# A decoder layer with sparse and dilated attention: six edits to what TensorE reads, and when

## The chip, the cores and the metric

One core of a Trainium2 chip runs the whole layer as one program. Its engines are TensorE (PE in the profile: matrix products, with its weight loads shown as PEld), VectorE (DVE), ScalarE (ACT), GpSimd (POOL) and SyncE (SP), which starts most DMA transfers. The metric is the device time of one execution in microseconds (us), the median of several runs.

## The reference, cut to what matters

The layer works on 512 tokens of 1024 channels, in float32: a half-step feed-forward block, a token mixer, and a second half-step feed-forward block, each between RMS norms.

```python
def token_mixer(h, ...):
    proj = h @ w_in                         # queries, keys, values, gates of all branches
    o_nsa = nsa_attention(...)              # compressed + selected + window branch, 8 heads
    o_dil = dilated_attention(...)          # 3 groups of 4 heads, dilation 1, 4, 16
    y_nsa = o_nsa.reshape(B, S, Q_NSA) @ w_nsa_o
    y_dil = o_dil.reshape(B, S, DIL_OUT) @ w_dil_o
    y = jax.nn.sigmoid(g_a) * y_nsa + jax.nn.sigmoid(g_b) * y_dil
    return y @ w_mix_out

def nsa_attention(...):
    ...
    p_cmp, _ = masked_softmax(s_c, dist_c >= 0)     # 31 compressed blocks
    o_cmp = jnp.einsum('bgrsc,bcgd->bsgrd', p_cmp, vc)
    ...
    return g[..., 0:1] * o_cmp + g[..., 1:2] * o_slc + g[..., 2:3] * o_win

def reference(x, ...):
    h = rms_norm(x, ffn1_pre)
    x = x + 0.5 * rms_norm(swiglu(h, ffn1...), ffn1_post)
    h = rms_norm(x, mix_pre)
    x = x + rms_norm(token_mixer(h, ...), mix_post)
    h = rms_norm(x, ffn2_pre)
    return x + 0.5 * rms_norm(swiglu(h, ffn2...), ffn2_post)
```

With 512 tokens all eight selected blocks are chosen, so the selected branch is plain causal attention, as the window branch is: the kernel runs two causal heads ("branches", br = 0 and 1) for each of 8 query heads, and a small compressed head beside them.

## The kernel before, in words

**Products.** Each float32 product is made of three matmuls in the 4-byte format fp32r: both operands are split into a high part (a cast on ScalarE, line 163) and the rest (a subtraction on VectorE, line 164), and `mm3` (lines 208 to 210) adds high times high, high times rest and rest times high. In the profile a matmul is written out<-moving,stationary. The stationary operand is loaded into the array ahead of its matmul (PEld); the moving operand streams through it, up to 512 columns. With `turn=True` the moving operand's two halves are read in turn, column 0 of the first half, column 0 of the second, and so on; the result then stands in that order in PSUM and is put right by the strided read of whoever takes it out (`from_turn`).

**Order of the work.** The program is traced in Python order; a scheduler then orders each engine's instructions by their place in the trace and by what its own model of time finds ready. `issue_after(i)` keeps what is traced in its block behind instruction i on i's engine; it is an order, not a wait. Tiles of one tag share a fixed number of buffers ("slots"); a new tile waits until an older one is read for the last time. The tag SP has 11 slots, raw (weights as they come from memory) 3, and PSUM's eight banks are shared as S 3, T 2, V 1, F 2.

**Sparse branch** (`nsa`, about 365 to 510 us). Sixteen turns n take one pair of head and branch each; the work of a turn is drawn out over three turns (LAG = 2). At every fourth turn two heads' queries are projected and split (`q_parts`). `cmp_pair` makes the compressed branch of two heads: 8 small score matmuls (line 1211), a softmax on VectorE and ScalarE, 4 transposes (line 1232), a split. `hb_probs` scales and transposes the probabilities of turn n - 2 (line 1275) into bank T and splits them into PT slots, in three portions: key tile 0, then key tiles 1 and 3 together, then key tile 2. `hb_scores` makes the scores of turn n into bank S (lines 1013 and 1014) and their softmax rows. `hb_values` (line 1290) multiplies values and probabilities of turn n - 2 for the key tiles 0, 1, 2, 3, of 512, 384, 256 and 128 query columns, once for the high part and once for the rest. At the second branch one more matmul (line 1364) adds the compressed branch, and `fold` (lines 1298 and 1299) adds the two 64-row halves of the bank. Units of the merge gates' projection are put between as filler.

**Dilated branch** (`dil`, about 510 to 698 us). Group 0 has dilation 1; groups 1 and 2 run on tokens in residue order, token 4n + r at place r, n. Queries and keys come from "lots" of block products (`lot_blocks`), whose summed operands (`mix_token_sums`) are held in the SP slots. The values of group 0 are projected from 620 us; those of groups 1 and 2 follow as one loop over eight k: the stationary operand is a quarter of the tokens, read with a step of four elements straight out of the normed input:

```python
xs = [x[k0 + j].rearrange("p (n r) -> p r n", r=4) for x in (self.xh, self.xl)]
for t in range(NT):
    self.mm3(banks[t], xs[0][:, t], xs[1][:, t], w[0][:, j], w[1][:, j], ...)
```

Meanwhile `factors` makes each group's share from the softmax sums (lines 1719 to 1734), and GpSimd scales all probabilities by it (line 1747). Then twelve items, four heads by three groups, are transposed (`transposed`, lines 1799 and 1812), split into SP slots, multiplied by the values (`values`, lines 1826 and 1827 for group 0, 1834 for the others) and added up (line 1839); the sparse branch's output products are filler between them. `dil_weights(0)`, the split of the first half of w_dil_o, is traced behind all items.

**End.** `ffn_down` ends with the rows of token tile 3: a square on ScalarE (line 216), the factor on VectorE and GpSimd (lines 225 and 229), the gain (line 955), two updates of 512 columns (line 927), and two stores of 256 KB on SP's queue (line 2139).

Of the kernel before, what the change touches and what calls it, by code (L numbers as in the profile page):

```python
# [17 lines left out]
OP = mybir.AluOpType  # L18
# [66 lines left out]
class Layer:  # L85
# [110 lines left out]
    def halves(self, v):  # L196

        return v.rearrange("p (h a c) -> p h a c", h=2, a=2)

    def rows_of(self, v):  # L200
# [553 lines left out]
    def ffn_down(self, first, E, later, kept, wd, td, post, finish, xsrc, aside, opened):  # L754
# [200 lines left out]
        nc.vector.tensor_mul(c[1], c[1], gain[0][0])  # L955
        update(3, (c[1], c22[1]), r)
        finish(3, gain[1])

# [327 lines left out]
    def hb_values(self, probs, br, half, out, first):  # L1286
        for kk in range(NT):
            v = self.vn[kk][:, 2 * br + half].rearrange("p h d -> p (h d)")
            for pi, pp in enumerate(probs[kk]):
                self.nc.tensor.matmul(out[:, kk * P:S], v, pp, start=first and kk == 0 and pi == 0, stop=False,  # L1290
                                      skip_group_check=True)

# [8 lines left out]
    def nsa(self, fillers, sums):  # L1301
# [32 lines left out]
        for n in range(len(heads) + LAG):  # L1334
            if n < len(heads) and n % 4 == 0:
                i = n // 4
                b, _ = self.proj_T(None, None, None, wq) if i == 0 else self.proj_T(self.wcols([(i * 64, 64), (256 + i * 64, 64)]))
                qs[i] = self.q_parts(b)
                if i:
                    cmps[i] = self.cmp_pair(i, qs[i])  # L1340
            m = n - LAG
# [4 lines left out]
            if n < len(heads):  # L1346
                i, half, br = heads[n]
                h = i + 4 * half
                if br == 0:
                    ws[h] = self.slot("W")  # L1350
                    nc.vector.tensor_scalar(ws[h], self.dm, -(2.0 ** -(h + 1)), None, op0=OP.mult)
                kb, ka = kparts[br]
                live[n] = self.hb_scores(qs[i][half], ka[half], kb, half, ws[h])
            if m >= 0:
                i, half, br = heads[m]
                with self.tc.issue_after(self.last_pool):
                    sums(m)
                if br == 0:
                    out = self.bank("V")
                    if half == 0:  # L1360
                        of = self.slot("x")
                self.hb_values(probs.pop(m), br, half, out, br == 0)
                if br == 1:
                    nc.tensor.matmul(out, self.vcs[half], cmps[i], start=False, stop=True, skip_group_check=True)
                    self.fold(of, half, out[0:64], out[64:128])
                    if half == 1:
                        self.oh.append(of)
# [190 lines left out]
    def dil(self, fillers, early_gates):  # L1558
# [216 lines left out]
        for k0 in range(0, KT, 2):  # L1775
            if k0 % 4 == 0:
                r = self.raw(wv[:, k0:k0 + 4], [4, S])
            w = self.wsplit(r[:, k0 % 4:k0 % 4 + 2], [2, S])
            if k0 == 2:
                factors()  # L1780
            for j in range(2):
                xs = [x[k0 + j].rearrange("p (n r) -> p r n", r=4) for x in (self.xh, self.xl)]
                for t in range(NT):
                    self.mm3(banks[t], xs[0][:, t], xs[1][:, t], w[0][:, j], w[1][:, j], k0 + j == 0, k0 + j == KT - 1,
                             turn=True)
# [34 lines left out]
        def values(g, hh, pieces, acc):  # L1820

            mm = nc.tensor.matmul
            if g == 0:
                out = self.bank("V")
                for n, (kk, qc, hi, lo) in enumerate(pieces):
                    mm(out[:, qc], value(g, kk, hh), hi, start=n == 0, stop=False, skip_group_check=True)
                    self.last_value = mm(out[:, qc], value(g, kk, hh), lo, start=False, stop=n == NT - 1, skip_group_check=True).ins
                nc.scalar.copy(acc, out)
                return
            for m, both in enumerate(pieces):  # L1830
                out = self.bank("S")
                for n in range(2):
                    c = slice(n * 256, (n + 1) * 256)
                    self.last_value = mm(out[:, c], value(g, 2 * m + n, hh), both[:, n].rearrange("p x q -> p (x q)"), start=True,
                                         stop=True).ins
                av = acc.rearrange("p (n r) -> p n r", r=4)[:, :, 2 * m:2 * m + 2]
                ov = out.rearrange("p (r x n) -> p x n r", r=2, x=2)
                for x in range(2):
# [11 lines left out]

        self.dh, self.dl = [], []
        items = [(hh, g) for hh in range(4) for g in range(3)]
        pend = {}
        for n in range(len(items) + 1):
            if n < len(items):
                hh, g = items[n]
                pend[n] = transposed(g, hh)
            with self.tc.issue_after(self.last_value if n == len(items) else self.last_trans):
                for _ in range(2 if n == 0 else 1):
# [31 lines left out]
    def mixer(self, post, finish, sums):  # L1891
# [89 lines left out]

        dil_weights(0)
        for d in range(KT):
# [137 lines left out]
    def run(self, out):  # L2121
        nc, a = self.nc, self.a
        self.xdram = self.tc.dram_tile([S, D], F32, name="xdram")
        self.x2dram = self.tc.dram_tile([S, D], F32, name="x2dram")
        NP = NF // 2
# [77 lines left out]
```

## Time and profile before

| | before |
|---|---|
| median of 3 runs | 1083.85 us (1083.21 to 1085.04) |
| the profiled execution | 1083.9 us, span 1081.8 us |
| TensorE busy, weight loads | 1060.2 us (98%), 974.6 us |
| VectorE, ScalarE, GpSimd busy | 915.0, 667.9, 246.4 us |
| mean granted clock of TensorE | 0.999 |
| memory read and written | 214.73 and 74.50 MB |

The span runs from the first to the last instruction of the program; the execution's own time is a little longer. Busy times of TensorE include the time that a matmul needs to run out of the array, which overlaps the next one, so the distance between starts says more than the busy share. In the groups, "x32 | 15.0, 478 | 2.2 <-ACT" is the count, the busy time in us, the mean duration in ns, and the idle time ahead of the group with what ended it. In the timeline each row has its start and its duration in us.

### The profile page before, as it was taken

How to read it: one execution, taken by the hardware profiler on the slowest of the kernel's cores; microseconds unless marked ns; L12 is line 12 of the kernel's file. 1: busy time of each engine (PE TensorE's matmuls, PEld its weight loads, DVE VectorE, ACT ScalarE, POOL GpSimd, SP SyncE). 2: the span in 40 equal slices, each digit the busy share in tenths (PEclk: the TensorE clock that was granted, in tenths of full speed). 3: DMA queues.
4: the chain of work that ended last, by engine and by line, in shares of the span. 5: the costliest groups of instructions: out<-in, count | busy, mean ns of one | idle time of the engine just before them, and what ended most of it. 6: DMA issues, size and time to landing. Idle time of an engine off the chain costs nothing. (4 is left out here: it accounts for less than half of the span.)

```text
span 1081.8 us, 19360 instructions
## 1 busy us (share of the span) xinstructions
PE 1060.2 (98%) x7166; PEld 974.6 (90%) x7166; DVE 915.0 (85%) x1563; ACT 667.9 (62%) x1196; POOL 246.4 (23%) x345
## 2 busy tenths in 40 slices
PE   9999999999999999999999999999999999999997
PEld 7899999988889977777899998888999999998886
DVE  6999999998787988787996746996888999989775
ACT  7465555567675777676797745754445555668462
POOL 0434445410021054454110039001101111000001
PEclk9999999999999999999999999999999999999999
DMA  9899999999962577886766642574387988579862
GB/s 351 259 273 312 284 299 294 303 315 351 355 225 87 195 263 174 263 187 204 166 196 224 206 119 99 180 263 162 131 276 203 261 248 229 152 248 301 301 203 105
DMA packets 87871, 250.65 MB, mean 232 GB/s; under 512 B 11777, under 2 KB 16993, under 8 KB 85089
## 3 DMA queue, kind: packets, MB, share of 16 engines
q1 hardware_dynamic: 67152, 180.40, 48.4%
q0 software_dynamic: 20192, 68.72, 25.5%
q8 instruction: 56, 0.92, 0.3%
q10 hardware_dynamic: 432, 0.30, 0.1%
q14 instruction: 39, 0.31, 0.1%
HBM read 214.73 MB, written 74.50 MB: 267 GB/s over the span
## 5 line engine op out<-in xcount | busy, mean ns | idle before, releaser
L164 DVE TENSOR_TENSOR wlo<-raw,whi 128x1024 fp32r<-128x1024 f32 (+1 forms) x216 | 261.8, 1217 | 79.9 <-ACT whi L163 77.2
L163 ACT CAST whi<-raw 128x1024 fp32r<-128x1024 f32 (+1 forms) x216 | 223.8, 1040 | 95.3 <-PE pb_F L209 17.2
L208 PE MATMUL pb_F<-xhl_t,whi 128*128 128x256 f32 (+1 forms) x320 | 104.7, 327 | 2.0 <-DVE KA_s L996 1.0
L209 PE MATMUL pb_F<-xhl_t,whi 128*128 128x256 f32 (+1 forms) x320 | 103.1, 322 | 0.0
L210 PE MATMUL pb_F<-xhl_t,wlo 128*128 128x256 f32 (+1 forms) x320 | 103.1, 322 | 0.0
L208 PE MATMUL pb_S<-xhl_t,whi 128*128 128x256 f32 (+1 forms) x280 | 82.2, 294 | 0.0
L209 PE MATMUL pb_S<-xhl_t,whi 128*128 128x256 f32 (+1 forms) x280 | 82.1, 293 | 0.0
L210 PE MATMUL pb_S<-xhl_t,wlo 128*128 128x256 f32 (+1 forms) x280 | 82.1, 293 | 0.0
L229 POOL TENSOR_TENSOR rs_t<-rs_t,mhalf_t 128x1 f32<-128x1 f32 x20 | 13.3, 666 | 249.5 <-DVE rs_t L225 249.5
L208 PEld LDWEIGHTS pb_F<-xhl_t,whi 128*128 128x128 f32 x320 | 61.0, 191 | 6.1 <-issue 1.6
L210 PEld LDWEIGHTS pb_F<-xhl_t,wlo 128*128 128x128 f32 x320 | 61.0, 190 | 3.3
L209 PEld LDWEIGHTS pb_F<-xhl_t,whi 128*128 128x128 f32 x320 | 61.0, 191 | 3.0 <-issue 0.2
L1266 POOL TENSOR_SCALAR SP_s<-SP_s,st_t 128x384 f32<-128x384 f32 (+2 forms) x48 | 49.1, 1053 | 55.5 <-PE pb_T L1232 11.6
L209 PE MATMUL pb_T<-xhl_t,whi 128*128 128x256 f32 x216 | 59.4, 275 | 0.0
L210 PE MATMUL pb_T<-xhl_t,wlo 128*128 128x256 f32 x216 | 59.4, 275 | 0.0
L208 PE MATMUL pb_T<-xhl_t,whi 128*128 128x256 f32 x216 | 59.4, 275 | 0.0
L163 ACT CAST whi<-tmp_t 128x1024 fp32r<-128x1024 f32 x36 | 36.5, 1057 | 30.2 <-DVE tmp_t L582 26.6
L210 PEld LDWEIGHTS pb_S<-xhl_t,wlo 128*128 128x128 f32 x280 | 53.6, 191 | 1.3
L208 PEld LDWEIGHTS pb_S<-xhl_t,whi 128*128 128x128 f32 x280 | 53.6, 191 | 1.3
L209 PEld LDWEIGHTS pb_S<-xhl_t,whi 128*128 128x128 f32 x280 | 53.6, 191 | 1.3
L208 PE MATMUL pb_T<-SP_s,whi 128*128 128x256 f32 x176 | 48.8, 277 | 1.5 <-ACT ring_s L1539 1.0
L210 PE MATMUL pb_T<-SP_s,wlo 128*128 128x256 f32 x176 | 48.7, 277 | 0.0
(930 smaller groups left out, 3713.4 us busy)
## 6 DMA issues: line engine op xcount, KB each, us to landing
raw<-in_gu_dram SPq DMA_DIRECT2D x64, 512.0 KB, 5.8
raw<-tdram SPq DMA_DIRECT2D x40, 512.0 KB, 5.0
PT_s<-in_d_dram POOLq DMA_DIRECT2D x66, 256.0 KB, 6.9
raw<-in_d_dram SPq DMA_DIRECT2D x30, 512.0 KB, 5.1
tdram<-in_d_dram POOLq DMA_DIRECT2D x18, 768.0 KB, 10.4
ldram<-in_w_in_dram POOLq DMA_DIRECT2D x12, 1024.0 KB, 10.5
tdram<-PT_s POOLq DMA_DIRECT2D x44, 256.0 KB, 5.9
raw<-in_w_in_dram SPq DMA_DIRECT2D x11, 1024.0 KB, 4.9
```

Of the source, the lines that this page charges most:

```text
L163: self.last_cast = self.nc.scalar.copy(dsthi, src).ins
L164: self.last_sub = self.nc.vector.tensor_sub(dstlo, src, dsthi.bitcast(F32)).ins
L208: mm(out, lhi, rhi, start=start, stop=False, skip_group_check=skip)
L209: mm(out, lhi, rlo, start=False, stop=False, skip_group_check=skip)
L210: self.last_mm = mm(out, llo, rhi, start=False, stop=stop, skip_group_check=skip).ins
L229: nc.gpsimd.tensor_tensor(out=r, in0=v, in1=self.mhalf, op=OP.pow)
L1266: self.last_pool = nc.gpsimd.tensor_scalar(pp, pp, st[:, 1, t:t + 1], None, op0=OP.mult).ins
```

## The change

Six edits, all to order or layout; the values computed are the same.

- **Tokens in residue order.** The two stationary operands of each k of the value projection of groups 1 and 2 are copied by ScalarE into SP slots in residue order, 16 copies of 128 x 512, and the matmuls read the copies.
- **Two rows in turn.** The probabilities of `hb_values`, of the compressed branch and of `values` are read as two rows in turn (in `hb_values` and group 0 the two halves of each tile of 128 columns, 64 elements apart; in groups 1 and 2 the high part and the rest, 128 apart). The outputs are unpicked where PSUM is read.
- **Value tile order.** `hb_values` takes the key tiles in the order 0, 1, 3, 2.
- **Compressed branch.** `cmp_pair` of the later head pairs is traced behind `hb_scores` of its turn instead of ahead of `hb_probs`.
- **Weight split.** The cast and the subtraction of `dil_weights(0)` are put behind those of the third item from the end as traced (`piece[-3]`, the tenth of twelve).
- **Last stores.** In the second feed-forward block the last token tile is updated in four pieces of 256 columns, second half first, each stored at once, on SP's and ScalarE's queues in turn.

```diff
@@ -196,6 +196,22 @@
     def halves(self, v):
 
         return v.rearrange("p (h a c) -> p h a c", h=2, a=2)
+
+    def tiles(self, v):
+
+        return v.rearrange("p (t a c) -> p t a c", a=2, c=64)
+
+    def tiles_in_turn(self, v):
+
+        return v.rearrange("p (t a c) -> p t c a", a=2, c=64)
+
+    def tiles_turned(self, v):
+
+        return v.rearrange("p (t c a) -> p t c a", a=2, c=64)
+
+    def tiles_from_turn(self, v):
+
+        return v.rearrange("p (t c a) -> p t a c", a=2, c=64)
 
     def rows_of(self, v):
 
@@ -953,8 +969,16 @@
         product(half(parts["O"], 256), "T4", None, c, False, True, settle, 6, list(HOLD_TAGS), between)
         r = factor(3, [square(3, c[1]), ms[3, 1]])
         nc.vector.tensor_mul(c[1], c[1], gain[0][0])
-        update(3, (c[1], c22[1]), r)
-        finish(3, gain[1])
+        if opened:
+            update(3, (c[1], c22[1]), r)
+            finish(3, gain[1])
+            return
+        for h, y in ((1, c22[1]), (0, c[1])):
+            x = self.x[6 + h]
+            for i in range(2):
+                o = slice(i * 256, (i + 1) * 256)
+                nc.vector.scalar_tensor_tensor(x[:, o], y[:, o], r, x[:, o], op0=OP.mult, op1=OP.add)
+                (nc.sync, nc.scalar)[i].dma_start(self.last_rows[:, h * S + i * 256:h * S + (i + 1) * 256], x[:, o])
 
 
     def wcols(self, segs):
@@ -1284,11 +1308,11 @@
         return out
 
     def hb_values(self, probs, br, half, out, first):
-        for kk in range(NT):
+        for kk in (0, 1, 3, 2):
             v = self.vn[kk][:, 2 * br + half].rearrange("p h d -> p (h d)")
             for pi, pp in enumerate(probs[kk]):
-                self.nc.tensor.matmul(out[:, kk * P:S], v, pp, start=first and kk == 0 and pi == 0, stop=False,
-                                      skip_group_check=True)
+                self.nc.tensor.matmul(self.tiles_turned(out[:, kk * P:S]), v, self.tiles_in_turn(pp),
+                                      start=first and kk == 0 and pi == 0, stop=False, skip_group_check=True)
 
     def fold(self, dst, half, top, bot):
 
@@ -1336,8 +1360,6 @@
                 i = n // 4
                 b, _ = self.proj_T(None, None, None, wq) if i == 0 else self.proj_T(self.wcols([(i * 64, 64), (256 + i * 64, 64)]))
                 qs[i] = self.q_parts(b)
-                if i:
-                    cmps[i] = self.cmp_pair(i, qs[i])
             m = n - LAG
             if m >= 0:
                 i, half, br = heads[m]
@@ -1351,6 +1373,8 @@
                     nc.vector.tensor_scalar(ws[h], self.dm, -(2.0 ** -(h + 1)), None, op0=OP.mult)
                 kb, ka = kparts[br]
                 live[n] = self.hb_scores(qs[i][half], ka[half], kb, half, ws[h])
+            if n < len(heads) and n % 4 == 0 and n:
+                cmps[n // 4] = self.cmp_pair(n // 4, qs[n // 4])
             if m >= 0:
                 i, half, br = heads[m]
                 with self.tc.issue_after(self.last_pool):
@@ -1361,8 +1385,9 @@
                         of = self.slot("x")
                 self.hb_values(probs.pop(m), br, half, out, br == 0)
                 if br == 1:
-                    nc.tensor.matmul(out, self.vcs[half], cmps[i], start=False, stop=True, skip_group_check=True)
-                    self.fold(of, half, out[0:64], out[64:128])
+                    nc.tensor.matmul(self.tiles_turned(out), self.vcs[half], self.tiles_in_turn(cmps[i]), start=False, stop=True,
+                                     skip_group_check=True)
+                    self.fold(self.tiles(of), half, *[self.tiles_from_turn(out[b:b + 64]) for b in (0, 64)])
                     if half == 1:
                         self.oh.append(of)
             if n < 2:
@@ -1779,7 +1804,11 @@
             if k0 == 2:
                 factors()
             for j in range(2):
-                xs = [x[k0 + j].rearrange("p (n r) -> p r n", r=4) for x in (self.xh, self.xl)]
+                xs = []
+                for x in (self.xh, self.xl):
+                    v = self.slot("SP", F32R).rearrange("p (r n) -> p r n", r=4)
+                    nc.scalar.copy(v, x[k0 + j].rearrange("p (n r) -> p r n", r=4))
+                    xs.append(v)
                 for t in range(NT):
                     self.mm3(banks[t], xs[0][:, t], xs[1][:, t], w[0][:, j], w[1][:, j], k0 + j == 0, k0 + j == KT - 1,
                              turn=True)
@@ -1823,18 +1852,19 @@
             if g == 0:
                 out = self.bank("V")
                 for n, (kk, qc, hi, lo) in enumerate(pieces):
-                    mm(out[:, qc], value(g, kk, hh), hi, start=n == 0, stop=False, skip_group_check=True)
-                    self.last_value = mm(out[:, qc], value(g, kk, hh), lo, start=False, stop=n == NT - 1, skip_group_check=True).ins
-                nc.scalar.copy(acc, out)
+                    o, hi, lo = self.tiles_turned(out[:, qc]), self.tiles_in_turn(hi), self.tiles_in_turn(lo)
+                    mm(o, value(g, kk, hh), hi, start=n == 0, stop=False, skip_group_check=True)
+                    self.last_value = mm(o, value(g, kk, hh), lo, start=False, stop=n == NT - 1, skip_group_check=True).ins
+                nc.scalar.copy(self.tiles(acc), self.tiles_from_turn(out))
                 return
             for m, both in enumerate(pieces):
                 out = self.bank("S")
                 for n in range(2):
                     c = slice(n * 256, (n + 1) * 256)
-                    self.last_value = mm(out[:, c], value(g, 2 * m + n, hh), both[:, n].rearrange("p x q -> p (x q)"), start=True,
-                                         stop=True).ins
+                    self.last_value = mm(out[:, c].rearrange("p (q x) -> p q x", x=2), value(g, 2 * m + n, hh),
+                                         both[:, n].rearrange("p x q -> p q x"), start=True, stop=True).ins
                 av = acc.rearrange("p (n r) -> p n r", r=4)[:, :, 2 * m:2 * m + 2]
-                ov = out.rearrange("p (r x n) -> p x n r", r=2, x=2)
+                ov = out.rearrange("p (r n x) -> p x n r", r=2, x=2)
                 for x in range(2):
                     nc.vector.tensor_add(av, ov[:, x], av)
 
@@ -1849,12 +1879,14 @@
             self.ol.append(lo)
 
         self.dh, self.dl = [], []
+        self.piece = []
         items = [(hh, g) for hh in range(4) for g in range(3)]
         pend = {}
         for n in range(len(items) + 1):
             if n < len(items):
                 hh, g = items[n]
                 pend[n] = transposed(g, hh)
+                self.piece.append((self.last_cast, self.last_sub))
             with self.tc.issue_after(self.last_value if n == len(items) else self.last_trans):
                 for _ in range(2 if n == 0 else 1):
                     next(fillers)
@@ -1979,7 +2011,8 @@
         def dil_weights(d):
             dil_w[d // 4] = self.wsplit(self.raw(wd[d // 4], [2, 512]), [2, 512])
 
-        dil_weights(0)
+        with tc.issue_after(self.piece[-3][0]), tc.issue_after(self.piece[-3][1]):
+            dil_weights(0)
         for d in range(KT):
             if d % 2 and EARLY <= d + 3 < KT:
                 nsa_w[(d + 3) // 2] = first_weights(d + 3)
@@ -2121,6 +2154,7 @@
     def run(self, out):
         nc, a = self.nc, self.a
         self.xdram = self.tc.dram_tile([S, D], F32, name="xdram")
+        self.last_rows = out[3 * P:4 * P]
         self.x2dram = self.tc.dram_tile([S, D], F32, name="x2dram")
         NP = NF // 2
         td = [self.tc.dram_tile([4, P, NP, S], F32, name=f"tdram{i}") for i in range(2)]
```

## The prediction

> **What bounds the kernel now.** First the page, lines 1 and 2, for the busiest engine and its clock; then the table by stage, for the stages that the change touches.
>
> ```profile
> span 1081.8 us, 19360 instructions
> PE 1060.2 (98%) x7166; PEld 974.6 (90%) x7166; DVE 915.0 (85%) x1563; ACT 667.9 (62%) x1196; POOL 246.4 (23%) x345
> PEclk9999999999999999999999999999999999999999
> ```
>
> ```profile
> 608.00:632.60 24.60, 24.07 (x216) 23.92 (x215) 13.94 (x40) 14.63 (x39) 0.00 (x0) 1.00 0.64 223
> 632.60:655.40 22.80, 22.80 (x98) 22.79 (x97) 11.92 (x28) 8.58 (x17) 15.93 (x19) 1.00 0.31 82
> 390.00:510.00 120.00, 115.96 (x664) 93.61 (x662) 95.57 (x288) 86.46 (x213) 58.47 (x66) 1.00 0.77 217
> ```
>
> TensorE (PE) is busy for 98% of the span at full clock, so time goes only where PE works faster or waits less. The columns of the table are PE, its weight loads, VectorE, ScalarE, GpSimd. At 632.6 to 655.4 us the values of the dilated groups 1 and 2 are projected: PE has no gap and weight loading is as busy as PE, while ScalarE is used for 8.58 of 22.80 us. At 390 to 510 us (the sparse branch) PE waits now and then: here a faster read is worth less than its face.
>
> The profiled execution took 1083.9 us, 2.1 us beyond its span; the median of the runs is 1083.85, so the sum is made from 1083.9.
>
> **Tokens copied into residue order (the value projection).** The stationary operand is read there with a step of four elements, 16 bytes. The groups of this stretch, the same matmul with a plain stationary operand, and two places of the timeline:
>
> ```profile
> L208 PE MATMUL pb_S<-whi,xhl_t 128*128 128x512 f32 x16 | 6.5, 407 | 0.0
> L210 PE MATMUL pb_S<-whi,xhl_t 128*128 128x512 f32 x16 | 6.4, 398 | 0.0
> L209 PEld LDWEIGHTS pb_S<-wlo,xhl_t 128*128 128x128 f32 x16 | 5.4, 335 | 0.0
> ```
>
> ```profile
> L208 PE MATMUL pb_S<-xhl_t,whi 128*128 128x512 f32 x48 | 18.2, 379 | 0.0
> L208 PEld LDWEIGHTS pb_F<-xhl_t,whi 128*128 128x128 f32 x320 | 61.0, 191 | 6.1 <-issue 1.6
> ```
>
> ```profile
> 639.80 0.40 PE L208 MATMUL pb_T<-whi,xhl_t 128*128 128x512 f32 x1
> 640.03 0.40 PE L209 MATMUL pb_T<-wlo,xhl_t 128*128 128x512 f32 x1
> 655.42 0.38 PE L208 MATMUL pb_F<-xhl_t,whi 128*128 128x512 f32 x1
> 655.63 0.38 PE L209 MATMUL pb_F<-xhl_t,whi 128*128 128x512 f32 x1
> ```
>
> A load takes 335 ns instead of 191, and the matmuls follow one another every 0.23 to 0.24 us instead of 0.21 to 0.22. The stage has 96 of them (8 k, 4 residues, 3 products) in 22.80 us, 237.5 ns each; at the plain rate the sum of durations says 379 instead of about 401, 22 ns less: 96 x 22 ns = 2.1 us. Bounds: nothing (the loads are slow for another reason) to 2.1 us; I take 2.1, since the plain rate returns at once at 655.42.
>
> The price is 16 ScalarE copies. The nearest rows are a copy of this size out of SBUF, and one that reads with a step of four (out of PSUM):
>
> ```profile
> L163 ACT CAST x_s<-x_s 128x512 fp32r<-128x512 f32 x4 | 2.5, 618 | 1.9 <-DVE SP_s L164 1.9
> L1539 ACT COPY ring_s<-pb_T x4: 573/589/592, 560.9 to 610.2; 128x512 f32<-128x512 f32 x4
> ```
>
> The step costs nothing there, so 16 x 0.62 = 9.9 us of ScalarE. It is idle for 10 us of the 24.6 before the stage and 14.2 of the 22.8 within it, the source is ready since the norm, and the eleven SP slots are free once the last lot's products have read their sums, so eight or more copies can run ahead of the first matmul: cost 0. If that cover is gone, the copies stand in front of PE, up to 9.9 us. They are also put ahead of the exponentials that feed the softmax factors, and GpSimd's scaling behind those has little room:
>
> ```profile
> 656.49 3.33 POOL L1747 TENSOR_SCALAR x_s<-x_s,gf_t 128x128 f32<-128x128 f32 x4
> 659.81 2.33 POOL L1747 TENSOR_SCALAR CP_s<-CP_s,gf_t 128x128 f32<-128x128 f32 x4
> 662.07 0.49 PE L1799 MATMUL pb_T<-ident_t,x_s 128*128 128x128 f32 x3
> 664.66 0.41 PE L1799 MATMUL pb_T<-ident_t,CP_s 128*128 128x128 f32 x2
> ```
>
> PE now takes x_s at 662.07, 2.2 us after its scaling ends at 659.82. Arriving 2.1 us sooner it just finds it done (0.1 us of room), and CP_s with 664.66 - 2.1 - 662.14 = 0.4 us. GpSimd is what is late next.
>
> **Probabilities read as two rows in turn.** The moving operand of the value matmuls is now read plainly. The groups by form, then a plain 512-column matmul of the opening that runs back to back, and a 256-column pair:
>
> ```profile
> L1290 PE MATMUL pb_V<-PT_s,V_s 128*128 128x512 f32 x32 | 15.0, 478 | 2.2 <-ACT PT_s L163 1.8
> L1290 PE MATMUL pb_V<-PT_s,V_s 128*128 128x384 f32 x32 | 10.5, 357 | 0.0
> L1290 PE MATMUL pb_V<-PT_s,V_s 128*128 128x128 f32 x32 | 5.4, 249 | 0.0
> L1290 PEld LDWEIGHTS pb_V<-PT_s,V_s 128*128 128x128 f32 x128 | 20.9, 188 | 11.2 <-ACT PT_s L163 8.0 <-DVE x_s L1299 0.9 <-DVE PT_s L164 0.6
> L1364 PE MATMUL pb_V<-CP_s,vcs_t 128*128 128x512 f32 x8 | 3.5, 444 | 0.0
> L2082 PE MATMUL pb_F<-xhl_t,wlo 128*128 128x512 f32 x8 | 3.2, 394 | 0.0
> ```
>
> ```profile
> L1834 PE MATMUL pb_S<-SP_s,KA_s x16: 278/282/287, 666.4 to 691.7; 128*128 128x256 f32 x16
> L209 PE MATMUL pb_T<-xhl_t,whi 128*128 128x256 f32 x216 | 59.4, 275 | 0.0
> ```
>
> 394 read plainly against 379 in turn is 15 ns for 512 columns. The sparse branch reads 16 x 2 x (512 + 384 + 256 + 128) + 8 x 512 = 45,056 columns, 88 times 512: 1.3 us. Upper end, if all that L1290 and L1364 show above 379 went: 32 x 99 + 8 x 65 ns = 3.7 us; but much of the 478 is the weight load that stands open after a wait for a cast (11.2 us of waits before the loads), which stays. Lower end 0: such a wait takes the gain. I take 0.9. The 32 dilated matmuls of L1834 lose 282 - 275 = 7 ns each, 0.2 us; L1826 and L1827 nothing. The results are unpicked while they leave PSUM, with a step of two, as the projections already do; cost 0, hidden on VectorE and ScalarE beside PE.
>
> Here a rule speaks against the change. The Trainium skill ("SBUF — State Buffer", section "Door 1: The DMA port swizzle") says that SBUF has 16-byte lines and that each access which crosses to a new line pays. By it the copy into residue order gains, but two rows in turn, a new line at each element, would be slower than a plain read; the rows have 379 against 394 the other way, at 512 and 1024 bytes between the rows. What no row has is the new distance, 64 elements or 256 bytes; I take it like the others.
>
> **Value tile order.** Tiles 1 and 3 come out of one cast, tile 2 out of the next; with 3 ahead of 2, PE has two more matmuls for tile 2's cast to hide in. Of the 11.2 us of waits most stand before tile 0, which doesn't move. Between 0 and 1.0 us; I take 0.3.
>
> **Compressed branch behind the scores.** No instruction is added; for i = 1 to 3 the branch's 8 score matmuls, 12 small VectorE operations, exponential and 4 transposes are queued behind the transposes and scores of the same turn.
>
> ```profile
> L1211 PE MATMUL pb_S<-kcs_t,Q_s 128*128 128x64 f32 x32 | 4.9, 276 | 0.7 <-DVE Q_s L1006 0.5 <-DVE Q_s L1007 0.2
> L1232 PE MATMUL pb_T<-ident_t,SP_s 128*64 128x128 f32 x16 | 2.5, 278 | 0.6 <-DVE SP_s L1228 0.6
> ```
>
> PE waits 1.3 us at these. The softmax rows go ahead on VectorE; its result is used three turns later, so nothing waits for it. The scores read the same Q_s, so part of the wait moves to them. Between -1.3 and +1.3 us (the same wait again, elsewhere); I take -0.7.
>
> **Weight split of w_dil_o.** Its cast and subtraction go behind those of the tenth of twelve pieces.
>
> ```profile
> 682.93 1.05 ACT L163 CAST whi<-raw 128x1024 fp32r<-128x1024 f32 x1 [0.16 <-PE pb_F L209]
> 685.03 0.30 PE L1812 MATMUL pb_T<-ident_t,PT_s 128*128 128x128 f32 x1 [0.76 <-DVE SP_s L164]
> 688.68 1.21 DVE L164 TENSOR_TENSOR wlo<-raw,whi 128x1024 fp32r<-128x1024 f32 x1
> 693.31 0.38 PE L208 MATMUL pb_F<-W_s,whi 128*128 128x512 f32 x1
> ```
>
> The cast stands ahead of a piece's cast and may be part of the 0.76 us wait; VectorE was busy too, so I take 0.2 of 0 to 0.76. It is used at 693.31, 3.4 us after the subtraction ends: no loss. Its load on SP's queue isn't moved; it holds one of three raw buffers 5 us longer at most.
>
> **Last stores.** Two updates of 512 columns and two stores on SP become four of 256, on SP's and ScalarE's queues in turn.
>
> ```profile
> 1077.28 0.75 DVE L927 SCALAR_TENSOR_TENSOR x_s<-of_s,rs_t,x_s 128x512 f32<-128x512 f32 x1
> 1077.94 0.75 DVE L927 SCALAR_TENSOR_TENSOR x_s<-pb_T,rs_t,x_s 128x512 f32<-128x512 f32 x1
> 1078.06 0.99 SPq L2139 DMA_DIRECT2D out_dram<-x_s  x2
> DMA to landing us min/median/max: 2.0/2.0/2.0
> ```
>
> VectorE's last piece ends when it did; each queue still issues two. Only the last landing can shrink: from 2.0 to 1.0 us if time goes with bytes, or grow by 0.3 if ScalarE's issue is later; I take -0.2. The Trainium skill (the same page, "The DMA setup-cost knee") gives about 2 us fixed plus bytes at 436 GB/s, 0.3 us for the half that is left out: an estimate.
>
> **Sum:** 2.1 + 0.9 + 0.2 + 0.3 + 0.7 + 0.2 + 0.2 = 4.6; 1083.9 - 4.6 = 1079.3 us.
>
> **Rivals.**
> GpSimd (or ScalarE's exponentials before it) sets the pace behind the projection: the 0.1 us of room speaks for it, that the copies can run early against it. 2.1 us given back: 1081.4. Chance 0.15.
> The sparse branch swallows its gains (0.9 + 0.3 + 0.7), since its casts release PE: for it the 11.2 us of waits, against it PE's 116 busy of 120 us. 1081.2. Chance 0.14.
> The strided load isn't what slows the projection, so the copies do nothing: 1081.4; against it the 335 ns. Chance 0.03.
> Slower: the copies come late, SP slots being held or ScalarE's queue full, and PE waits for each. All 16 exposed: 1079.3 + 9.9 = 1089.2; it decides from 4.6 / 0.62, seven to eight exposed copies. Chance 0.06.
> Slower: two rows only 256 bytes apart are slow. At the strided load's price, 335 - 191 = 144 ns for 128 columns, 352 times: 51 us, 1130; it decides from 16 ns for 128 columns (5.7 us with the 1.1 us of gain lost). It is what the skill's rule on lines would give. Chance 0.05.
> More waits go than I count (upper ends of order, branch, split and stores): 1076.8. Chance 0.09.
>
> **Numbers.** The forecast has 0.48. The range, 1076.3 to 1083.3, reaches from the larger gain to the two likelier of the cases near 1081.3 together (1079.3 + 2.1 + 1.9); the two slower rivals stay out. A measurement can tell 0.2%, 2.2 us: faster is below 1081.7. From the forecast 0.48, the larger gain 0.09 and two thirds of the cases at 1081.3 (0.21) comes 0.78; same 0.12; slower 0.10.
>
> **What would show it.** Right: the projection's matmuls at 379 ns and its loads near 191, stage near 20.7 us; L1290's 512-column group below 470; the first waits at the compressed branch gone; no wait at 685; last landing under 2.0. Wrong: PE waiting for GpSimd's x_s or CP_s behind the projection, PE waiting for ScalarE's copies, or a new wait for Q_s at the scores.

## The result, and the profile after

| | before | after |
|---|---|---|
| median of 5 runs, us | 1083.85 (1081.50 to 1085.04) | 1090.15 (1087.89 to 1092.13) |
| the profiled execution: its own time / span, us | 1083.9 / 1081.8 | 1090.15 / 1088.4 |
| ratio | | 1.0062, 95% interval 1.0049 to 1.0075 |

The change makes the kernel 0.62% slower: 6.7 us, where 4.6 us faster was forecast. First the head of the page, then three rows of the table by stage, cut where something happens (columns as in the prediction: PE, its weight loads, VectorE, ScalarE, GpSimd, each with its instructions; granted clock; DMA share; GB/s):

```profile
span 1088.4 us, 19406 instructions
PE 1059.4 (97%) x7166; PEld 971.5 (89%) x7166; DVE 915.8 (84%) x1565; ACT 687.5 (63%) x1212; POOL 247.4 (23%) x345
```

```profile
617.80:623.37 5.57, 0.04 (x2) 0.01 (x1) 1.59 (x10) 5.57 (x14) 0.00 (x0) 0.80 0.54 188
623.37:627.97 4.60, 4.60 (x21) 4.60 (x22) 4.35 (x11) 2.31 (x5) 0.00 (x0) 0.50 0.38 124
...
639.03:659.83 20.80, 20.80 (x99) 18.23 (x98) 12.63 (x28) 15.83 (x22) 14.81 (x14) 1.00 0.29 89
```

TensorE's busy time fell by only 0.8 us, to 1059.4, and its span grew by 6.6. In the first stretch it does nothing while ScalarE is busy throughout; in the second it is busy, but with 21 matmuls of 256 columns in 4.6 us, at half the clock. The third is the value projection with plain loads: its 96 matmuls run from 639.03 to 659.75 us, 20.7 us, where the kernel before took 22.8. That part came out as forecast, to a tenth of a microsecond.

The timeline of the first stretch (start, duration, engine, line, operation, tiles; in brackets the idle time before it and what ended it), first ScalarE, then PE; the third fence is the same place of the kernel before:

```profile
617.17 4.11 ACT L1810 CAST SP_s<-xhl_t 128x512 fp32r<-128x512 f32 x4
621.19 0.40 ACT L1044 ACTIVATE CP_s<-CP_s,dst_t 128x128 f32<-128x128 f32 x1
...
622.74 0.57 ACT L1576 ACTIVATE ring_s<-pb_T 128x512 f32<-128x512 f32 x1
```

```profile
623.37 0.58 PE L224 MATMUL pb_T<-SP_s,whi 128*128 128x256 f32 x1 [5.53 <-ACT ring_s L1576]
```

```profile
618.45 0.59 ACT L1551 ACTIVATE ring_s<-pb_T 128x512 f32<-128x512 f32 x1
...
619.09 0.38 PE L208 MATMUL pb_T<-SP_s,whi 128*128 128x256 f32 x1 [0.54 <-ACT ring_s L1551]
```

L1810 is the copy into residue order; L1576 (L1551 before) is the copy of lot 3's product out of bank T, which PE needs back. In ScalarE's timeline, four copies stand ahead of the exponentials that belong to lot 3's work (621.19 is the first of four), and these ahead of the release of bank T. PE does not wait for a copy: it waits for what stands behind the copies, 5.53 us instead of 0.54. And a copy does not take the 0.62 us of the forecast. The view of its line (shortest, median and longest in ns, first and last start):

```profile
L1810 ACT CAST SP_s<-xhl_t x16: 1083/1354/1577, 608.1 to 648.8; 128x512 fp32r<-128x512 f32 x16
```

The copies that stay for the time of the projection push its own ScalarE work back, the casts of `x_s` among it, and with those VectorE's subtractions; GpSimd's scaling runs beside them and is slower. The same seven scalings (six of 256 columns and one of 128; a merged row shows the first one's shape) in the timeline, first in the kernel before, then here, and then PE's wait for one of the next:

```profile
641.69 6.56 POOL L1747 TENSOR_SCALAR PT_s<-PT_s,fac_t 128x256 f32<-128x256 f32 x7
```

```profile
647.23 10.57 POOL L1772 TENSOR_SCALAR PT_s<-PT_s,fac_t 128x256 f32<-128x256 f32 x7
...
667.24 0.33 PE L1828 MATMUL pb_T<-ident_t,x_s 128*128 128x128 f32 x1 [0.58 <-POOL x_s L1772]
```

The path, by setting each PE instruction beside the one of the same rank in the trace of before (times are those of before): after is 0.61 us late at 386 us, where none of the six edits has run yet, 1.17 us ahead at 508 (the sparse branch), 0.71 ahead at 618, 6.44 behind at 624, 4.43 behind at 659 (the projection gave 2.1 back), 7.5 behind at 667 (GpSimd), 5.9 at 680, 7.31 at 721, and 6.56 at the end.

### The profile page after: what moved, and what is told of

It reads as the page before. It is cut to its first block, busy times and chain, and to the rows that moved or that the text cites. A ratio compares the mean times of both kernels' runs of the same rounds, so it can differ in the third digit from the quotient of the medians.

```text
span 1088.4 us, 19406 instructions
## 1 busy us (share of the span) xinstructions
PE 1059.4 (97%) x7166; PEld 971.5 (89%) x7166; DVE 915.8 (84%) x1565; ACT 687.5 (63%) x1212; POOL 247.4 (23%) x345
```

## Experiments

The theory after this reading: the copies' price in ScalarE's queue makes the loss, by a long wait, a slow clock behind it and a late GpSimd; the other five edits give what was forecast. The rival: reading two rows in turn, or another of the five, costs time. Ratios are to the kernel before, timed on the same chip, with 95% intervals; 0.001 is 1.1 us.

**1. Without the copies.**

```
-  nc.scalar.copy(v, x[k0 + j].rearrange("p (n r) -> p r n", r=4))   # and its slot
+  xs = [x[k0 + j].rearrange("p (n r) -> p r n", r=4) for x in (self.xh, self.xl)]
```

> The change without the copies into residue order, the other five edits kept. Theory (ScalarE's queue: the copies stand ahead of lot 3's exponentials and of the copy that frees bank T, PE waits 5.5 us for it, then works 2 us slower, then waits 2 us more for GpSimd): the loss goes with the copies, and what is left is the 2.5 us that the prediction gave the other edits: 1083.85 - 2.5 = 1081.4 us (1080.5 to 1083.5), no PE gap over 1 us near 620 us. Rival (reading two rows in turn, or another of the five, costs time): 1086 us or more.

1082.34 us against 1082.24: 0.9997 (0.9985 to 1.0009). The loss goes with the copies, but the gain of 2.5 us is not there. Its trace has it and loses it: PE is 3.2 us ahead of the kernel before at 685 us (0.4 of them before the first edit runs, at 386 us) and 0.9 us ahead at 722, after this wait in the timeline (before: 0.50 us):

```profile
720.13 0.48 PE L225 MATMUL pb_T<-wlo,PT_s 128*128 128x512 f32 x1 [1.68 <-DVE wlo L164]
```

So one more edit costs time, and late: experiments 6, 7, 13 and 14.

**2. The copies alone.** The kernel before with the loop of L1807 to L1811 in it.

> The kernel before with the copies into residue order alone. Theory: 1083.85 - 2.1 (the projection) + 5.0 (the longer gap before the P7 product) + 2.1 (the clock behind it) + 2.2 (waits for GpSimd) = 1091 us (1088 to 1093). Rival (the loss needs another edit): 1082 to 1085 us.

1091.67 us, 1.0090 (1.0072 to 1.0108): the copies alone cost 9.7 us, more than the whole change. The wait for the copy out of bank T is 5.54 us here too.

**3. The copies turned round.** Each reads plainly and writes with a step.

```
-  nc.scalar.copy(v, x[k0 + j].rearrange("p (n r) -> p r n", r=4))
+  nc.scalar.copy(v.rearrange("p r n -> p n r"), x[k0 + j].rearrange("p (n r) -> p n r", r=4))
```

> The changed kernel with each copy turned round: it reads plainly and writes with a step of 128 elements, instead of reading with a step of four elements and writing plainly; every instruction stands where it did in its queue. If the step on the read side makes a copy 1.1 to 1.6 us and a step on the write side costs nothing, a copy takes 0.62 us, the eight copies ahead of bank T's release take 8 x 0.6 = 4.8 us less, and the time falls to 1083 to 1085 us. If any step costs the same: 1090 us, copies at 1.1 to 1.6 us as before.

1085.31 us, 1.0033 (1.0019 to 1.0047): half of the loss is gone, though the step on the write side is not free either, and the gap is still 4.15 us. The view of the line:

```profile
L1810 ACT CAST SP_s<-xhl_t x16: 1071/1127/1142, 607.8 to 644.5; 128x512 fp32r<-128x512 f32 x16
```

The turned copy takes 1.13 us wherever it stands. The copy that reads with the step varies: the four at 617.17 above, with PE standing still, follow one another every 1.03 us; others take up to 1.58.

**5. Plain copies in the same places** (the price is changed, the place is not). This kernel leaves the reordering out, so it multiplies other tokens; its work is otherwise the same.

```
+  nc.scalar.copy(v, x[k0 + j].rearrange("p (r n) -> p r n", r=4))   # no reordering
```

> The changed kernel with its 16 copies made plain, in the same places of ScalarE's queue: the tokens are not brought into residue order, so the values of groups 1 and 2 are those of other tokens. It parts the copies' price from their place. If the price was the fault (1.1 to 1.6 us where the prediction had 0.62): a copy takes 0.62 us, the eight copies ahead of bank T's release take 8 x 0.5 = 4 us less than the turned ones, whose gap before the P7 product was 4.1 us, so at most 1 us of gap is left over the 0.5 us that was there before; the time is 1080 to 1082 us. If the place was the fault, whatever a copy costs: a gap over 2 us stays, with the slow stretch behind it, 1084 us or more.

1081.71 us, 0.9991 (0.9981 to 1.0002). The view of the line, and the gap in the timeline:

```profile
L1810 ACT CAST SP_s<-xhl_t x16: 605/618/628, 607.3 to 641.2; 128x512 fp32r<-128x512 f32 x16
```

```profile
618.29 0.38 PE L224 MATMUL pb_T<-SP_s,whi 128*128 128x256 f32 x1 [1.50 <-ACT ring_s L1576]
```

618 ns: the price that the prediction took is that of a plain copy. At that price the same places leave a gap of 1.50 us instead of 5.53, and the loss is gone.

**4 and 9. The place.** Copies held behind named ScalarE instructions, so that none stands ahead of the release of bank T near 620 us; in 4 only the eight high parts, in 9 all sixteen. The cut is that of 4; 9 names more places.

```
+  with self.tc.issue_after(self.lot_end if n == 0 else keeps[1] if n < 3 else self.last_exp):
       nc.scalar.copy(v, xs[0])
```

> The changed kernel with the high parts alone copied (8 copies, not 16; the low part is read with its step, as before the change), and each copy held behind a named instruction of ScalarE: one behind lot 3's last copy, two behind the second tile of group 0's values, five behind the exponentials of the softmax factors. Theory of the queue: no long gap near 620 us; 64 of the 96 loads are plain, 1.4 us: 1081.4 - 1.4 = 1080.0 us, or 1081.4 if GpSimd's scaling sets the pace behind the projection. Rival (the copies themselves slow the chip, wherever they stand): 1085 us or more.

1080.24 us, 0.9984 (0.9973 to 0.9995): eight stepped copies fit, and the gap near 620 us is 0.54 us again.

> The changed kernel, all six edits, with the 16 copies (read with the step, 1.1 to 1.6 us each) held behind named instructions of ScalarE: two behind the copy that frees bank T for the next product, one behind lot 3's last copy, two behind the second and one behind the third tile of group 0's values, ten behind the softmax factors' exponentials. It changes the place and leaves the price. Theory: the gap near 620 us falls to 0.5 us and the clock stays; 16 copies of about 1.4 us are 22 us of ScalarE, hardly less than it has free from 619 us to the end of the stage, so PE waits for the last of them or for GpSimd's scaling, 1 to 4 us: 1081 to 1085 us, 5 us or more under the changed kernel's 1090. If the price alone decides: 1087 us or more, PE waiting for copies within the projection.

1089.22 us, 1.0053 (1.0037 to 1.0068): my theory of the place missed. The gap near 620 us is gone (0.52 us), but sixteen stepped copies of 1.49 us do not fit behind it. Ten of them, the first six below, fill ScalarE to 651 us, what it owes the end of the projection comes late, and PE stands still from 656.65 us, before the transposes that need bank T back (ScalarE's timeline, then two rows of the table by stage):

```profile
636.16 8.80 ACT L1816 CAST SP_s<-xhl_t 128x512 fp32r<-128x512 f32 x6
...
660.00 0.69 ACT L1781 CAST V_s<-pb_T 128x256 fp32r<-128x256 f32 x2
```

```profile
656.65:661.87 5.22, 0.00 (x0) 0.03 (x1) 4.77 (x10) 2.95 (x8) 5.22 (x7) 0.91 0.45 151
661.87:666.30 4.43, 4.43 (x14) 3.88 (x15) 1.34 (x3) 1.06 (x2) 4.43 (x8) 0.50 0.33 118
```

The profile names GpSimd's CP_s for that wait, but the rows at its end speak for VectorE (a row each of VectorE, GpSimd and PE's weight loads):

```profile
661.31 0.42 DVE L1782 TENSOR_TENSOR V_s<-pb_T,V_s 128x256 fp32r<-128x256 f32 x1
...
660.39 1.46 POOL L1772 TENSOR_SCALAR CP_s<-CP_s,gf_t 128x128 f32<-128x128 f32 x1
...
661.84 0.18 PEld L1847 LDWEIGHTS pb_T<-ident_t,PT_s 128*128 128x128 f32 x1 [5.59 <-issue]
```

The load starts at 661.84, 0.1 us after the subtraction that reads V_s out of bank T ends, and before GpSimd's scaling ends at 661.85. That subtraction follows ScalarE's casts of V_s, which come at 660.00. So it is bank T again, held by late work of ScalarE and of VectorE behind it. The wait is about the same size at another place, and again half a clock behind it.

For the stepped copy, then, the place only says where the price is paid: 1.0062 in the old places, 1.0053 in the new ones. For the cheaper turned copy the place counts: 1.0033 in the old places (experiment 3), 0.9977 in the new ones with the same six edits (experiment 14 below). Neither price nor place alone gives the gain; a plain copy, at 0.62 us, takes the loss away where it stands (experiment 5).

**8. The low parts on VectorE**, the high parts on ScalarE, placed, w_dil_o's split in its old place.

> The sixth kernel with the low parts copied too, on VectorE, held behind group 0's subtractions and behind the softmax factors' last product; the high parts stay on ScalarE as there. All 96 loads of the projection are plain: 0.7 us less than the sixth kernel if VectorE's copies fit in the 10 us that it has free in the stage (a copy at 0.6 to 0.7 us, 8 x 0.65 = 5.2 us): about 1078.2 us. If the step of four costs VectorE as it costs ScalarE (1.1 to 1.6 us each, 9 to 12 us), weight splits come late and PE waits: 1079 to 1082 us.

1084.35 us, 1.0021 (1.0012 to 1.0030). VectorE pays less for the step, but GpSimd pays beside it (its first scaling took 0.61 us in the kernel before); the view of the line, then GpSimd's timeline:

```profile
L1816 DVE CAST SP_s<-xhl_t x8: 743/857/967, 624.9 to 641.8; 128x512 fp32r<-128x512 f32 x8
```

```profile
634.58 3.76 POOL L1772 TENSOR_SCALAR PT_s<-PT_s,fac_t 128x128 f32<-128x128 f32 x1 [49.64 <-DVE fac_t L1759]
...
639.97 10.60 POOL L1772 TENSOR_SCALAR PT_s<-PT_s,fac_t 128x256 f32<-128x256 f32 x7
```

PE then waits 2.64 us for GpSimd's x_s at 660 us. The first of these scalings lies beside four of VectorE's copies, the next seven beside subtractions and one more copy. In the changed kernel the slow scalings lie beside VectorE's delayed subtractions. Experiment 9 speaks against the rival that ScalarE's stepped copies slow GpSimd themselves: from 639.98 us its ScalarE is full of them and VectorE does nothing until 645.94, and the seven scalings take 6.01 us:

```profile
639.98 6.01 POOL L1772 TENSOR_SCALAR PT_s<-PT_s,fac_t 128x256 f32<-128x256 f32 x7
```

So it is VectorE's work that slows GpSimd, by the rows; no run changed the subtractions alone. The Trainium skill ("GPSIMD Engine Reference", "1. Specifications") says that GpSimd shares its SBUF interfaces with VectorE, with contention for VectorE's instructions that have two SBUF inputs or run in a 2-port mode. The subtractions have two such inputs and agree with it; in which mode the copies ran no trace shows.

**10. Turned and placed**, w_dil_o's split in its old place: experiment 9's places, experiment 3's copy.

> The same places, with the copies turned round (plain read, step on the write side: 1.13 us each) and w_dil_o's split in its old place: 18 us of ScalarE, which fits. All 96 loads plain. If nothing else waits: the sixth kernel's 1079.97 less the 0.7 us of the low parts' loads, 1079.3 us. If GpSimd's scaling is what is late next (its first 16 scalings took 14.5 us without copies, 17 with plain or turned ones, 19 with stepped ones): 1080 to 1081.5 us, with PE waiting for x_s of GpSimd behind the projection.

1079.55 us, 0.9962 (0.9950 to 0.9974): faster than both kernels, by 4.1 us against the kernel before. No wait of 0.2 us or more for GpSimd is left; the projection runs from 629.89 to 650.6 us, and a copy takes 1.12 us (median), as in experiment 3; the view of the line:

```profile
L1816 ACT CAST SP_s<-xhl_t x16: 1087/1124/1177, 616.2 to 642.5; 128x512 fp32r<-128x512 f32 x16
```

**6, 7, 13 and 14. The weight split of w_dil_o.** Four pairs of kernels differ in this alone:

```
-  dil_weights(0)
+  with tc.issue_after(self.piece[-3][0]), tc.issue_after(self.piece[-3][1]):
+      dil_weights(0)
```

> The fourth kernel of the first four (high parts copied, copies held) with the first weight split of w_dil_o put back in its old place. There PE waited 1.85 us for a wlo of w_mix_out at 718 us, and w_dil_o's load went out at 687 us instead of 675. If the moved split holds up the raw buffers and so w_mix_out's weights: the wait falls to about 0.5 us, and the time from 1080.2 to about 1078.9 us (1078 to 1079.7). Rival (the loads of gates and w_mix_out set the pace of that stage, however early PE gets there): the wait stays, 1080.2 us within 0.5.

> The kernel before with four edits: two rows in turn, the value tile order, the compressed branch, the last stores; no copies, and w_dil_o's split in its old place. If the moved split gave back what the others gain: 1082.3 - 1.4 = 1080.9 us (1080.3 to 1081.6), the wait for wlo at 720 us falls from 1.7 to about 0.5 us. If the loads there give it back in any case: 1082.3 us.

> The kernel before with the first weight split of w_dil_o moved, alone. The prediction gave it -0.2 us. The first and the seventh kernel, which differ in this alone, had ratios of 0.9997 and 0.9978, and by their traces the move saves 1.2 us of waits near 675 us and costs 2.4 us of waits for w_mix_out's weights near 720 us. If that is the split: 1.0 to 2.0 us slower than the kernel before, ratio 1.001 to 1.002, w_mix_out's first load out 4 us or more later, PE waiting 1.5 us or more for wlo near 721 us. If those waits belong to PE's arriving early there: ratio 1.000 or below.

> The tenth kernel (all 16 copies turned and placed) with the split of w_dil_o in its new place again, so all six edits in it. If the split is worth a loss of 1 to 2 us: 1080.5 to 1081.5 us, ratio 0.997 to 0.998 where the tenth had 0.9962. If it is worth nothing: 0.996.

| the rest of the kernel | split in its old place | split moved |
|---|---|---|
| before | 1 | 1.0008 (0.9997 to 1.0019), experiment 13 |
| four edits | 0.9978 (0.9968 to 0.9988), experiment 7 | 0.9997 (0.9985 to 1.0009), experiment 1 |
| four edits, high parts copied | 0.9974 (0.9964 to 0.9984), experiment 6 | 0.9984 (0.9973 to 0.9995), experiment 4 |
| four edits, turned copies | 0.9962 (0.9950 to 0.9974), experiment 10 | 0.9977 (0.9966 to 0.9988), experiment 14 |

Each time the moved split is slower, by 0.8 to 1.9 thousandths, 1 to 2 us; some single intervals touch, the four pairs have one sign. Where it goes, in the timeline: the loads on SP's queue in the kernel before, then in experiment 13, with ScalarE, VectorE and PE behind them.

```profile
675.36 0.33 SPq L147 DMA_DIRECT2D raw<-in_w_dil_o_dram  x1
...
689.96 0.33 SPq L147 DMA_DIRECT2D raw<-in_w_mix_out_dram  x1
```

```profile
689.29 0.33 SPq L147 DMA_DIRECT2D raw<-in_w_dil_o_dram  x1
...
696.38 2.35 SPq L147 DMA_DIRECT2D raw<-in_w_mix_out_dram  x2
...
715.60 0.63 ACT L1935 ACTIVATE SP_s<-SP_s 128x512 f32<-128x512 f32 x1 [4.39 <-DMA SP_s<-gdram]
716.14 1.03 ACT L163 CAST whi<-raw 128x1024 fp32r<-128x1024 f32 x1
717.07 0.61 ACT L163 CAST Q_s<-SP_s 128x512 fp32r<-128x512 f32 x1
...
717.72 0.69 DVE L164 TENSOR_TENSOR Q_s<-SP_s,Q_s 128x512 fp32r<-128x512 f32 x1 [3.03 <-ACT Q_s L163]
...
721.33 1.22 DVE L164 TENSOR_TENSOR wlo<-raw,whi 128x1024 fp32r<-128x1024 f32 x1
...
722.60 0.48 PE L209 MATMUL pb_T<-wlo,PT_s 128*128 128x512 f32 x1 [2.71 <-DVE wlo L164]
```

The load of w_dil_o moved with its split: it goes out 14 us later, and w_mix_out's first load 6.4 us later behind it. ScalarE's casts change places with it (a weight's cast now stands ahead of Q_s), VectorE waits 3.03 us for Q_s, and the wlo that PE needs at 721 us comes out last. The waits near 675 us that the move takes away (0.74 and 0.39 us) are paid twice here. This profiled execution is the slowest of the experiment's eleven, 1087.24 us against a median of 1083.92, and half a clock follows the wait, from 723.64 to 727.05 us; in the other kernels with the moved split the same wait is 0.8 us (experiment 14) to 1.85 us (experiment 4). The loads go out late in all of them.

**11 and 12. The other terms, taken apart.** 11 reads two rows in turn and changes nothing else; 12 has the value tile order and the compressed branch.

> The kernel before with probabilities read as two rows in turn, alone. The prediction's terms are 0.9 us (sparse branch) and 0.2 us (dilated values): 1.1 us under the kernel before, a ratio of 0.9990; bounds 0 to 3.7 us. In the trace PE is 0.9 to 1.5 us earlier at 508 us than at 390 us, against the kernel before; the 512-column values take about 460 ns instead of 478. Rival (the sparse branch's casts swallow the gain): ratio 1.000.

1083.31 us, 0.9999 (0.9990 to 1.0007). By the two traces PE gains 0.33 us from 386 to 508 us and 0.17 us more by 691 us. The value groups are faster, but most of it is swallowed; the groups by form:

```profile
L1306 PEld LDWEIGHTS pb_V<-PT_s,V_s 128*128 128x128 f32 x128 | 20.7, 189 | 11.4 <-ACT PT_s L163 8.0 <-DVE x_s L1315 0.9 <-DVE PT_s L164 0.7
...
L1306 PE MATMUL pb_V<-PT_s,V_s 128*128 128x512 f32 x32 | 14.5, 463 | 2.3 <-ACT PT_s L163 1.9
```

The 512-column matmul takes 463 ns instead of 478; the 8.0 us of waits for ScalarE's cast are what they were.

> The kernel before with the two moves in the sparse branch alone: the value tile order and the compressed branch behind the scores. The prediction's terms are 0.3 and 0.7 us: 1.0 us under the kernel before, ratio 0.9991. The trace of the change without copies says otherwise: PE's waits between 386 and 515 us sum to 4.1 us there and 3.9 us before, so the waits have only moved: no difference, ratio 1.000, PE within 0.4 us of the kernel before at 508 us.

1081.02 us, 0.9980 (0.9971 to 0.9990): 2.1 us faster. My expectation was wrong: I had added up PE's own gaps, and they had not shrunk. The gain is in the loads' waits, which the profile books as PE's busy time; between 386 and 508 us PE gains 1.6 us. First the loads of the compressed branch from 385 to 515 us, before and in experiment 12, then the value loads' group and the table's row for the stage:

```profile
L1211 PEld LDWEIGHTS pb_S<-kcs_t,Q_s 128*128 128x128 f32 x32 | 4.2, 191 | 2.5 <-issue 1.2 <-DVE Q_s L1006 1.2
L1232 PEld LDWEIGHTS pb_T<-ident_t,SP_s 128*64 128x64 f32 x16 | 1.4, 111 | 1.8 <-DVE SP_s L1228 1.2 <-issue 0.6
```

```profile
L1211 PEld LDWEIGHTS pb_S<-kcs_t,Q_s 128*128 128x128 f32 x32 | 4.0, 192 | 0.7 <-DVE st_t L1019 0.5
L1232 PEld LDWEIGHTS pb_T<-ident_t,SP_s 128*64 128x64 f32 x16 | 1.4, 111 | 1.2 <-DVE SP_s L1228 1.0 <-issue 0.3
...
L1290 PEld LDWEIGHTS pb_V<-PT_s,V_s 128*128 128x128 f32 x128 | 21.0, 189 | 10.8 <-ACT PT_s L163 5.9 <-DVE PT_s L164 1.6 <-ACT ring_s L1401 1.1
```

```profile
390.00:508.00 118.00, 113.89 (x659) 93.57 (x658) 94.61 (x289) 87.61 (x214) 59.73 (x67) 1.00 0.76 215
```

The compressed branch's loads wait 1.9 us instead of 4.3. The value loads wait less for ScalarE's cast, 5.9 us instead of 8.0, but for others more: 10.8 us in all, where it was 11.2. So by these rows most of the gain is the compressed branch's; the two edits were not run apart. In the same 118 us there are 659 matmuls instead of 652.

## Why the prediction was wrong, point by point

- **Copies into residue order: the step that failed.** "The step costs nothing there, so 16 x 0.62" used a copy out of PSUM to price a copy out of SBUF with a step of 16 bytes. Measured: 1.08 to 1.58 us, median 1.35, so 16 copies are 21.7 us of ScalarE and not 9.9. The row for the true form was not in the trace, and the nearest was of another memory; both ends of that price should have stood in the text. The rule that the prediction itself quoted from the Trainium skill ("SBUF — State Buffer", "Door 1: The DMA port swizzle") was applied there to what PE reads, and not to the copy, each of whose elements lies on a line of its own. For the copy the trace agrees with it (1.35 us against 0.62); for the rows it does not.
- **"Eight or more copies can run ahead of the first matmul: cost 0."** They did run ahead: that was the damage. Idle time of ScalarE over a stretch was taken for room in its queue. Up to 620 us the idle pieces before were of 1.1 and 1.5 us, in front of work that others wait for, and the copies went ahead of that work two and four at a time. The rival "the copies come late" had a time near the truth (1089.2) by luck, by another way: PE waited 5.53 us for the release of bank T, not for copies.
- **The clock behind the wait** was in no term: 21 matmuls 213 ns apart instead of 112, 2.1 us.
- **GpSimd "is what is late next"**: right, and more than late. PE waited for x_s four times, 2.2 us; the scaling also became slower itself.
- **The projection, -2.1**: right. 20.7 us against 22.8, matmuls of 379 ns.
- **Two rows in turn, -0.9 and -0.2**: too large alone, 0.33 and 0.17 in the trace, nothing that the time can tell. The reading is faster, as the rows said; neither in time nor in the groups is the 256-byte distance slow, so that rival falls.
- **Value tile order and compressed branch, -0.3 and -0.7**: too small, 1.6 us in the trace and 2.1 in the time. The 1.3 us that the prediction counted at the compressed branch are PE's own gaps; the waits of its loads, 4.3 us, were not looked at. With the rows the four edits give 0.9978, 2.4 us, where the prediction's terms say 2.3: right in the sum by luck, since the shares were wrong.
- **w_dil_o's split, -0.2**: wrong in sign, +1 to +2 us. "Its load on SP's queue isn't moved" was the failed step: the load is issued by the same call and went out 14 us later.
- **Last stores, -0.2**: nothing. From the start of the last row's first update to the end of the span it is 4.5 us before and 4.6 after; "VectorE's last piece ends when it did" failed: four updates of 256 columns take 1.67 us where two of 512 took 1.41. The landing hardly followed the bytes, 1.9 us from the issue where it was 2.0, so what the smaller stores win is eaten. The timeline after:

```profile
1083.83 0.88 DVE L980 SCALAR_TENSOR_TENSOR x_s<-of_s,rs_t,x_s 128x256 f32<-128x256 f32 x2
...
1084.63 0.87 DVE L980 SCALAR_TENSOR_TENSOR x_s<-pb_T,rs_t,x_s 128x256 f32<-128x256 f32 x2
```

## What to carry to other kernels

A copy put on an engine with idle time is not free because the engine is idle on average: look at what stands behind it in that engine's queue, and price it by a row of the same memory and the same step, or carry both ends of the price into the range. Moving a weight split moves its load too, past everything else on the DMA queue that shares its buffers. And where the same reordering can be done by reading plainly and writing with a step, try that side: with all six edits and the same places, the copy took 1.12 us instead of 1.49, and 1.0053 (experiment 9) became 0.9977 (experiment 14). The places were needed too: the same copy in the old ones gave 1.0033 (experiment 3).

## What the runs showed of the hardware

The slow clock behind a wait comes in pieces of one length. In experiment 3 PE resumes at full rate after 4.15 us of waiting, falls to half of it at 621.92 us, and is back at 625.33:

```profile
621.80 0.32 PE L224 MATMUL pb_T<-SP_s,whi 128*128 128x256 f32 x1
621.92 0.42 PE L225 MATMUL pb_T<-SP_s,whi 128*128 128x256 f32 x1
...
625.12 0.37 PE L225 MATMUL pb_T<-V_s,whi 128*128 128x256 f32 x1
625.33 0.28 PE L226 MATMUL pb_T<-SP_s,wlo 128*128 128x256 f32 x1
```

That is 3.41 us. In experiment 5 the wait is only 1.50 us, and from 619.06 to 622.48 us, 3.42 us, the matmuls again follow one another every 213 ns instead of 112. In the changed kernel the granted clock is 0.50 from 621.10 to 627.92 us, twice that length; 2.3 us of it fall into the wait. In experiment 1 a wait of 1.68 us at 720 us is followed by no slow matmul, and in experiment 4 one of 1.85 us at 718 us.

The Trainium skill ("TensorE: Matmul & The Clock Gate", Part 1) has a window of 3413 ns that runs freely, a rate that is set by how busy PE has been, and the slow rate after at least one idle window. The length agrees; but no window was idle in experiment 5, where 1.50 us of waiting in 3.41 were enough. Why such waits differ in their price the runs leave open. That a wait is split between two windows does not explain it: in experiment 4, counted in steps of 3.413 us back from the next change of its clock (1075.05 us), 1.55 of the 1.85 us lie in one step.

So a wait of 1.5 us or more may cost up to 1.7 us beyond itself, half of a window, for each window that it slows; a wait of 0.5 us never did here.
